# The output stage of a hybrid attention and retention block: vector, scalar and GpSimd work in written order, with lags between squares, root and scalings

## Chip, cores and metric

The kernel runs on one core of one Trainium2 chip. The metric is device time in microseconds (us) of one execution.

## What is computed

The reference is one layer of an encoder block on 2048 tokens of width 1024, in float32: an RMS norm, one wide input projection, chunked attention with a relative bias (branch A), chunkwise retention with a group norm (branch B), a gated sum of both branches, an output projection, a residual, and a last RMS norm. The change touches the end:

```python
mixed = sigmoid(m_a) * branch_a + sigmoid(m_r) * branch_r
x = x + jnp.einsum('bsd,de->bse', mixed, w_out)
return rms_norm(x, final_gain)   # x * rsqrt(mean(x*x) + 1e-6) * final_gain
```

## The kernel before

**Jobs and chunks.** All dense projections run in one stream of jobs (`p0, g0, p1, g1, ba0, ba1, br0, br1, out`). The last is `out`, the output projection: eight chunks of 256 tokens. `br1` ahead of it makes the last part of the gated sum.

**Products.** A chunk of `out` is a 2x2 block product in seven block products (a Strassen form) instead of eight. The table PRODUCTS (line 227) gives for product n its resident operand R[m], its streamed operand and its PSUM bank: 0 and 3 add into bank x, 4 and 6 into z, 1 is y, 2 is v, 5 is w. The streamed operand of 0, 3 and 6 is a block of the loaded `raw` tiles, that of 4, 1, 2, 5 a difference t1, t2, t3, t4 of such blocks, made on GpSimd (`sum`, line 332). Every operand is split into a high part `wh` (a cast on ScalarE) and the remainder `wl` (a subtraction, on VectorE, for products 2 and 5 on GpSimd; `make`, line 294). One product is 12 matmuls: high times high, high times remainder, remainder times high, for four slices. It needs `wh` at its first matmul and `wl` at its third.

**Order of products.** `ORDERS` (line 48) has the orders: "s" for chunk 0, "o" for chunks 1 to 6, "l" for chunk 7. In "o" and "l" product 4 follows product 0. In "s" of the kernel before product 3 does: both write bank x, so product 3 waits until ScalarE has copied product 0's result out (`u2`, line 381). Product 6 adds into bank z, so it waits until VectorE has read z into `c22` (line 394), for which v must be there.

**Epilogue of a chunk.** `product` (lines 369 to 398) combines the banks into four 128x512 results on VectorE; `ep_out` (line 1207) takes each: VectorE adds the residual into the tile `xr`, ScalarE squares it and sums the squares (`jk`, line 1217), GpSimd multiplies by the gain (`fg`, line 1218). When a chunk has its four sums, VectorE computes the inverse root in a chain of 13 instructions on tiles of 128x2 (lines 196 to 211 and 1227), and ScalarE scales the four `fg` tiles (line 1235), which SyncE's DMA queue writes out. In chunk 7 the root and scalings run for each half as soon as its two squares are there, and half of the scalings are VectorE's.

**What sets the order.** Work is written out by step: a product is four steps, and `later(n, fn)` (line 244) puts `fn` n steps further on. Operands are prepared three products ahead (`AHEAD`, `prime`). Matmuls and SyncE's DMAs always keep the written order. ScalarE, VectorE and GpSimd go through `Sometimes` (line 148): while `strict[0]` is true they keep the written order, otherwise a scheduler that works with estimated durations orders each engine's instructions. Line 1787 sets it to false before `ba0`, so `ba`, `br` and `out` are ordered by the scheduler. While it is false, `make` writes the remainder right behind the cast, and the differences t1 to t3 all belong to product 0 ("loose" in `SUM_AT`). Each engine runs its instructions in its order, and one that waits holds all behind it, a DMA issue on ScalarE's queue (`raw`) included.

**The start of `out`.** The operands R[0], R[1], R[3] are in place when `out` begins. R[4], R[5], R[2], R[6] still hold operands of `br1` until its last four products (n = 4 to 7 of chunk 3) are done; after each of them `place_wo` (line 1183) overwrites one, with four casts on ScalarE and four remainders (VectorE three, GpSimd one). `raw` has three buffers; chunks 0 and 1 need four, so that the fourth load waits until t3 of chunk 0 is made.

Of the kernel before, what the change touches and what calls it, by code (L numbers as in the profile page):

```python
# [21 lines left out]
P = 128  # L22
SEQ = 2048
DM = 1024
# [6 lines left out]
T = 256  # L31
WIN = 640
ROPE_BASE = 10000.0
NORM_EPS = 1e-6
GN_EPS = 1e-5
MASK = 1e30
RSQRT_MAGIC = 1597463007.0
# [6 lines left out]
ORDERS = {"p": (0, 4, 1, 2, 3, 5, 6), "g": (0, 1, 3, 2, 4, 5, 6)}  # L44
FRONT = (0, 3, 5, 1, 2, 4, 6)
ORDERS["f"] = LAST = (0, 3, 1, 2, 4, 5, 6)

ORDERS["s"], ORDERS["o"], ORDERS["l"] = (0, 3, 4, 1, 2, 5, 6), (0, 4, 1, 2, 3, 5, 6), (0, 4, 1, 2, 5, 6, 3)
AHEAD = 3
PARTS = 8  # L50
RAWS = 3
# [21 lines left out]
def hybrid_kernel(  # L73
# [24 lines left out]
    small = ctx.enter_context(tc.tile_pool(name="small", bufs=4))  # L98
# [5 lines left out]
    def r32(ap):  # L104
        return ap.bitcast(F32)
# [40 lines left out]
    strict = [True]  # L146

    class Sometimes(Ordered):
# [3 lines left out]
    pe, act, dve, pool = Ordered(nc.tensor), Sometimes(nc.scalar), Sometimes(nc.vector), Sometimes(nc.gpsimd)  # L152
# [43 lines left out]
    def rsqrt(v, y, tmp, hv):  # L196

        dve.tensor_scalar(tmp.bitcast(I32), v.bitcast(I32), 1, None, ALU.logical_shift_right)
        dve.tensor_scalar(
            y.bitcast(I32), tmp.bitcast(I32), -1.0, RSQRT_MAGIC, ALU.mult, ALU.add  # L200
        )
        dve.tensor_scalar(hv, v, -0.5, None, ALU.mult)
        if v.shape[-1] == 1:
            for _ in range(3):
                dve.scalar_tensor_tensor(tmp, y, hv, y, ALU.mult, ALU.mult)
                dve.scalar_tensor_tensor(y, tmp, 1.5, y, ALU.add, ALU.mult)
            return
        for _ in range(3):
            dve.tensor_tensor(tmp, y, hv, ALU.mult)
            dve.tensor_tensor(tmp, tmp, y, ALU.mult)  # L210
            dve.scalar_tensor_tensor(y, tmp, 1.5, y, ALU.add, ALU.mult)
# [45 lines left out]
    def put(lag, dst, src):  # L257

        later(lag, lambda: dma(dst, src))
# [10 lines left out]
    class Chunk:  # L270
# [54 lines left out]

# [3 lines left out]
    }  # L329

    class Strassen(Chunk):
# [17 lines left out]
                later(1 + 3 * k, lambda q=q: load(q))  # L349

        def sums(self, n):
            if self.b is None and self.raw:
# [112 lines left out]
    def dense(jobs):  # L465
        chunks = [ch for job in jobs for ch in job.chunks]
        following = dict(zip(chunks, chunks[1:]))
        starts = [k for k, (job, ch, n) in enumerate(seq) if isinstance(ch, Plain) and ch.at(n)[2] == 0]
        count, begins = {}, {}
        for at, (job, ch, n) in enumerate(seq):  # L470
            if isinstance(ch, Strassen):
                begins.setdefault(ch, at)
        sooner = {at - lead: (ch, [j]) for ch, at in begins.items() for j, lead in enumerate(RAW_LEADS)}
        one, two_, three = jobs[2].chunks[:3]
        for ch in (one, two_, three):
            for lead in RAW_LEADS:
                sooner.pop(begins[ch] - lead)
        two_.raw, three.raw = [], []
        at = begins[one]
        sooner[at - 9], sooner[at - 6] = (one, [0]), (one, [1])  # L480

        first_out = jobs[-1].chunks[0]
        at = begins[first_out]
        for lead in RAW_LEADS:
            sooner.pop(at - lead)
        sooner[at - 6], sooner[at - 4] = (first_out, [0]), (first_out, [1])
        operands = {begins[ch] - 2: ch for ch in begins if ch.job.before}
        for at, (job, ch, n) in enumerate(seq):
# [664 lines left out]
    wo = {}  # L1153
# [26 lines left out]
        later(10, sums)  # L1180
        later(13, rest)

    def place_wo(m):
        for k in range(4):
            def low(k=k):
                eng = pool if k == 2 else dve
                eng.tensor_tensor(R[m][1][:, k, :], wo[m, k], r32(R[m][0][:, k, :]), ALU.subtract)

            later(1 + k, lambda k=k: act.copy(R[m][0][:, k, :], wo[m, k]))
            later(2 + k, low)  # L1190
# [5 lines left out]
    rows_out = {}  # L1196

    def before_out(c, i, j):
        t = 2 * c + j
# [7 lines left out]
    def ep_out(c, i, j, src, ps):  # L1207

        t = 2 * c + j
        xr, fg = jobs[-1].chunks[c].got.pop((i, j))  # L1210

        dve.scalar_tensor_tensor(xr, src, 0.25, xr, ALU.mult, ALU.add)
# [3 lines left out]
        junk = E(f"jk_{t}_{i}", BF16)  # L1216
        act.activation(junk, xr, AF.Square, scale=DM ** -0.5, accum_out=fs[:, j, i:i + 1])
        pool.tensor_tensor(fg, xr, fg, ALU.mult)
        tiles[j, i] = fg
        last = c == SEQ // T - 1  # L1220

        js = [j] if last and {(j, 0), (j, 1)} <= set(tiles) else [0, 1] if not last and len(tiles) == 4 else []
        if not js:
            return
        n = len(js)
        ft, fr, tm, hv = (small.tile([P, n], F32, tag=f"f{k}_{n}", bufs=2, name=f"f{k}_{t}") for k in range(4))
        dve.scalar_tensor_tensor(ft, fs[:, js[0]:js[-1] + 1, 0], NORM_EPS, fs[:, js[0]:js[-1] + 1, 1], ALU.add, ALU.add)
        rsqrt(ft, fr, tm, hv)
        for k, j in enumerate(js):
            t = 2 * c + j  # L1230
            for f in range(2):
                if f and last:
                    dve.tensor_scalar(tiles[j, f], tiles[j, f], fr[:, k:k + 1], None, ALU.mult)
                else:
                    act.mul(tiles[j, f], tiles[j, f], fr[:, k:k + 1])
                dst = out[0, t * P:(t + 1) * P, 512 * f:512 * f + 512]
                if t == SEQ // P - 2 and not f:
                    act.dma_start(dst, tiles[j, f])
                else:
                    put(6, dst, tiles[j, f])  # L1240


    def attention(s, sbp, ps_wide):
# [450 lines left out]
    end, at = {}, 0  # L1694
# [4 lines left out]
    def hook(name, c, n, fn):  # L1699
        hooks.setdefault((name, c, n), []).append(fn)  # L1700
# [10 lines left out]
        hook("br1", *divmod(1 + 6 * k, 8), lambda k=k: fill_wo(k))  # L1711


    for n, m in ((4, 4), (5, 5), (6, 2), (7, 6)):
        hook("br1", 3, n, lambda m=m: place_wo(m))

    stream = [dense(jobs)]
    seq.extend((job, ch, n) for job in jobs for ch, n in job.seq)
    for j in (jobs[0], jobs[2]):
# [143 lines left out]
```

## Time and profile before

| | us |
|---|---|
| median of 3 runs (lowest, highest) | 1993.12 (1991.28, 1993.23) |
| profiled execution | 1991.35 |
| its span | 1989.6 |
| PE busy | 1913.1 (96%) |
| VectorE, GpSimd, ScalarE busy | 1422.6, 994.7, 936.9 |
| stage `out`, first to last matmul | 1801.42 to 1979.83 |
| from there to the end of the span | 9.77 |

The profile is one execution on the chip. PE is TensorE, PEld its weight loads, DVE VectorE, ACT ScalarE, POOL GpSimd, SP the SyncE queue. Rows of the timeline give start, duration, engine, line and instruction, and in brackets how long the engine had been idle and what released it. Rows that keep the written order carry the line of the wrapper, 142. A matmul's shown duration overlaps the next one's: what counts is the distance between starts.

### The profile page before, as it was taken

How to read it: one execution, taken by the hardware profiler on the slowest of the kernel's cores; microseconds unless marked ns; L12 is line 12 of the kernel's file. 1: busy time of each engine (PE TensorE's matmuls, PEld its weight loads, DVE VectorE, ACT ScalarE, POOL GpSimd, SP SyncE). 2: the span in 40 equal slices, each digit the busy share in tenths (PEclk: the TensorE clock that was granted, in tenths of full speed). 3: DMA queues.
4: the chain of work that ended last, by engine and by line, in shares of the span. 5: the costliest groups of instructions: out<-in, count | busy, mean ns of one | idle time of the engine just before them, and what ended most of it. 6: DMA issues, size and time to landing. Idle time of an engine off the chain costs nothing.

```text
span 1989.6 us, 30295 instructions
## 1 busy us (share of the span) xinstructions
PE 1913.1 (96%) x9616; PEld 1586.9 (80%) x9616; DVE 1422.6 (72%) x2582; ACT 936.9 (47%) x1893; POOL 994.7 (50%) x799
## 2 busy tenths in 40 slices
PE   6899999999999999999999999999999999999997
PEld 4777878888888887778788888888888878887775
DVE  7887878677765668888886677765656654557776
ACT  6454454566654555343334555554555322224443
POOL 2343544555546675544543444544665115557664
PEclk9999999999999999999999999999999999999999
DMA  4576796756549988667676555555998999876663
GB/s 148 158 263 185 226 300 204 208 152 183 164 122 280 294 247 279 194 226 217 189 224 199 165 162 171 151 149 157 274 280 279 337 344 339 305 247 206 202 202 109
DMA packets 335055, 434.85 MB, mean 219 GB/s; under 512 B 30040, under 2 KB 194544, under 8 KB 334896
## 3 DMA queue, kind: packets, MB, share of 16 engines
q1 hardware_dynamic: 269296, 368.68, 58.5%
q10 hardware_dynamic: 65600, 64.24, 10.6%
q8 instruction: 77, 1.26, 0.3%
q14 instruction: 82, 0.67, 0.1%
HBM read 288.21 MB, written 144.60 MB: 218 GB/s over the span
## 4 chain that ended last, share of the span: by engine, by line
PE 73%; DVE 14%; DMA 5%; issue 4%; ACT 3%; POOL 1%; SPq 1%; ACTq 0%; DVEq 0%; POOLq 0%
PE ps_g_z L142 6%; PE ps_g_x L142 6%; PE ps_p_z L142 6%; PE ps_p_x L142 5%; PE po L142 4%; PE wide L142 4%; PE ps_g_y L142 3%; PE ps_g_v L142 3%; PE ps_g_w L142 3%; PE tp L142 3%; PE o L142 3%; PE ps_p_y L142 2%; PE ps_p_w L142 2%; PE ps_p_v L142 2%; DVE u_p L142 2%
## 5 line engine op out<-in xcount | busy, mean ns | idle before, releaser
L142 POOL TENSOR_SCALAR pr<-pr,rsum 128x640 f32<-128x640 f32 (+4 forms) x128 | 96.0, 750 | 225.9 <-DVE ptl L142 105.8
L142 POOL TENSOR_TENSOR t_p<-raw_p,t_p 128x512 f32<-128x512 f32 x50 | 73.5, 1470 | 147.6 <-DVE wl_p L142 125.7
L142 PE MATMUL ps_g_z<-r,wh_g 128*128 128x512 f32 x448 | 143.2, 401 | 2.1 <-DVE c_g L142 1.9
L142 DVE CUSTOM_DVE_ANT_0 pr<-wide,bt 128x640 f32<-128x640 f32 (+4 forms) x128 | 94.3, 737 | 71.0 <-PE wide L142 63.2
L142 PE MATMUL ps_p_z<-r,wh_p 128*128 128x512 f32 x448 | 141.2, 396 | 3.2 <-DVE c_p L142 2.8
L142 PE MATMUL ps_g_x<-r,wh_g 128*128 128x512 f32 x448 | 143.1, 400 | 0.9 <-ACT u_g L142 0.9
L142 PE MATMUL ps_p_x<-r,wh_p 128*128 128x512 f32 x448 | 141.6, 397 | 1.6 <-ACT u_p L142 1.5
L142 ACT ACTIVATE pr<-pr,mn 128x640 f32<-128x640 f32 (+4 forms) x128 | 98.1, 766 | 84.9 <-DVE mn L142 84.9
L142 DVE TENSOR_TENSOR ptl<-tp,pth 128x384 fp32r<-128x384 f32 x168 | 95.9, 573 | 41.0 <-ACT pth L142 40.7
L142 ACT CAST pth<-tp 128x384 fp32r<-128x384 f32 x168 | 84.7, 515 | 70.3 <-PE tp L142 64.8
L142 POOL TENSOR_TENSOR sl<-sm,sh 128x512 fp32r<-128x512 f32 x64 | 88.8, 1387 | 49.3 <-ACT sh L142 28.8
L142 DVE TENSOR_TENSOR wl_p<-t_p,wh_p 128x512 fp32r<-128x512 f32 x112 | 104.3, 932 | 2.1 <-ACT wh_p L142 2.1
L142 PEld LDWEIGHTS ps_p_x<-r,wh_p 128*128 128x128 f32 x448 | 83.4, 190 | 19.9 <-ACT u_p L142 2.4
L142 PEld LDWEIGHTS ps_p_z<-r,wh_p 128*128 128x128 f32 x448 | 81.8, 188 | 20.1 <-issue 4.8
L142 POOL TENSOR_TENSOR wl_g<-t_g,wh_g 128x512 fp32r<-128x512 f32 x56 | 75.1, 1341 | 43.0 <-ACT wh_g L142 41.0
L142 DVE TENSOR_TENSOR sm<-sr,dm 128x512 f32<-128x512 f32 x64 | 44.1, 689 | 73.4 <-PE sr L142 35.3
L142 PE MATMUL wide<-ka,qa 128*128 128x512 f32 (+2 forms) x448 | 94.2, 326 | 2.3 <-DVE mn L142 2.3
L142 PEld LDWEIGHTS tp<-ident,pr 128*128 128x128 f32 x560 | 71.3, 140 | 27.5 <-POOL pr L142 2.2
L142 PE MATMUL po<-pth,va 128*128 128x256 f32 x336 | 93.0, 297 | 0.0
L142 ACT CAST wh_p<-t_p 128x512 fp32r<-128x512 f32 x112 | 69.2, 620 | 48.7 <-PE ps_p_z L142 22.5
L142 PE MATMUL tp<-ident,pr 128*128 128x128 f32 x560 | 89.0, 273 | 2.9 <-POOL pr L142 1.6
L142 PEld LDWEIGHTS wide<-ka,qa 128*128 128x128 f32 x448 | 75.3, 188 | 19.2 <-DVE mn L142 7.7
(886 smaller groups left out, 6060.4 us busy)
## 6 DMA issues: line engine op xcount, KB each, us to landing
raw_g<-in_w_in_dram ACTq DMA_DIRECT2D x56, 512.0 KB, 5.3
raw_p<-in_w_in_dram ACTq DMA_DIRECT2D x50, 512.0 KB, 6.2
qa<-qas SPq DMA_DIRECT2D x128, 128.0 KB, 3.0
qr<-qrs SPq DMA_DIRECT2D x128, 128.0 KB, 4.5
vr<-vrs SPq DMA_DIRECT2D x64, 256.0 KB, 5.5
ka<-kas SPq DMA_DIRECT2D x40, 256.0 KB, 3.6
va<-vas SPq DMA_DIRECT2D x40, 256.0 KB, 3.0
kds<-kdt_k SPq DMA_DIRECT2D x32, 256.0 KB, 4.3
```

Source lines behind the costliest of these rows:

```text
L142: return tc.keep_in_program_order(op(*a, **k))
```

## The change

- From `br1`, chunk 3, after n = 2 on, `strict[0]` is true again: ScalarE, VectorE and GpSimd keep the written order to the end. With it the remainders are written four steps after the casts, and t1 to t4 are spread by three new rows of `SUM_AT`.
- Order "s" has product 4 before product 3. The two `raw` loads of chunk 0 are written 8 and 5 products ahead instead of 6 and 4.
- `ep_out` is split: residual, then squares one step later, then the root (one function for all chunks, 12 instructions, its iterate `tiny` in one PSUM bank of the pool of z and w) three to six steps later, the four scalings eight to eleven steps later, output DMAs four steps after each instead of six. Chunk 7 is no longer scaled by halves: all four scalings follow its fourth square, two on ScalarE with their DMAs on ScalarE's queue, two on VectorE.
- `place_wo` takes a first step and a spacing: (1, 1) for R[4], R[5], (2, 2) for R[2], (3, 2) for R[6]; remainders two steps behind casts.

```diff
-ORDERS["s"], ... = (0, 3, 4, 1, 2, 5, 6), ...
+ORDERS["s"], ... = (0, 4, 3, 1, 2, 5, 6), ...
...
+        "s": {0: ("t1",), 3: ("t2",), 1: ("t3",), 2: ("t4",)},
+        "o": {0: ("t1", "t2"), 4: ("t3",), 3: ("t4",)},
+        "l": {0: ("t1", "t2"), 4: ("t3",), 2: ("t4",)},
...
-        sooner[at - 6], sooner[at - 4] = (first_out, [0]), (first_out, [1])
+        sooner[at - 8], sooner[at - 5] = (first_out, [0]), (first_out, [1])
...
+        def added():
+            dve.scalar_tensor_tensor(xr, src, 0.25, xr, ALU.mult, ALU.add)
+            later(1, squares)
+        def squares():
+            act.activation(junk, xr, AF.Square, scale=DM ** -0.5, accum_out=fs[:, j, i:i + 1])
+            pool.tensor_tensor(fg, xr, fg, ALU.mult)
...
+            if len(tiles) == 4:
+                finish()
+        def finish():
+            if not tiny:
+                tiny.append(TR("tiny"))
+            y = tiny[0][:, 0:2]
...
+            later(3, first)
+            for n in range(3):
+                later(4 + n, lambda n=n: newton(n))
+            for k in range(4):
+                later(8 + k, lambda k=k: scaled(k // 2, k % 2))
+        added() if ps else later(1, added)
...
+    hook("br1", 3, 2, lambda: strict.__setitem__(0, True))
-        hook("br1", 3, n, lambda m=m: place_wo(m))
+        hook("br1", 3, n, lambda n=n, m=m: place_wo(m, *((1, 1) if n < 6 else (n - 4, 2))))
```

What this does to the engines' order is shown at two places. In the names, the first number behind `out` is the chunk, the second the product or the bank; `fg_0_1` belongs to token tile 0, half 1.

ScalarE, in the second chunk (chunk 1), before: the four scalings of chunk 0 stand ahead of the cast for product 5.

```order
L298 CAST wh_out_1_3_20269<-raw_out_1_1_20013 128x512
L381 COPY u2_out_1_20265<-ps_out_1_x_20247 128x512
L1235 ACTIVATE fg_0_0_19991<-fg_0_0_19991,f1_1_20224 128x512
L1235 ACTIVATE fg_0_1_20034<-fg_0_1_20034,f1_1_20224 128x512
L1235 ACTIVATE fg_1_0_20060<-fg_1_0_20060,f1_1_20224 128x512
L1235 ACTIVATE fg_1_1_20009<-fg_1_1_20009,f1_1_20224 128x512
L298 CAST wh_out_1_5_20290<-t4_out_1_20267 128x512
L298 CAST wh_out_1_6_20308<-raw_out_1_1_20013 128x512
```

The same place after the change:

```order
L142 COPY u2_out_1_20249<-ps_out_1_x_20225 128x512
L142 CAST wh_out_1_3_20255<-raw_out_1_1_20009 128x512
L142 CAST wh_out_1_5_20281<-t4_out_1_20198 128x512
L142 ACTIVATE fg_0_0_19987<-fg_0_0_19987,fr_0_20233 128x512
L142 ACTIVATE fg_0_1_20029<-fg_0_1_20029,fr_0_20233 128x512
L142 ACTIVATE fg_1_0_20053<-fg_1_0_20053,fr_0_20233 128x512
L142 ACTIVATE fg_1_1_20006<-fg_1_1_20006,fr_0_20233 128x512
L142 CAST wh_out_1_6_20307<-raw_out_1_1_20009 128x512
```

The cast for product 5 has moved ahead of the scalings; the cast for product 6 still follows them.

GpSimd, around the start of `out`, before: t2 and t3 of chunk 0 stand ahead of the additions `gr` of `br1`, chunk 3.

```order
L340 TENSOR_TENSOR t2_out_0_19945<-raw_out_0_1_19923,t1_out_0_19943 128x512
L340 TENSOR_TENSOR t3_out_0_19947<-raw_out_0_0_19885,raw_out_0_1_19923 128x512
L1148 TENSOR_TENSOR gr_6_2_19806<-gr_6_2_19806,ta_6_2_19807 128x512
L1148 TENSOR_TENSOR gr_6_3_19849<-gr_6_3_19849,ta_6_3_19850 128x512
L1187 TENSOR_TENSOR r41_90<-ws2_2_19631,r40_89 128x512
```

After the change t3 stands behind three of these additions and one remainder of R[4]:

```order
L1151 TENSOR_TENSOR gr_6_2_19806<-gr_6_2_19806,ta_6_2_19807 128x512
L142 TENSOR_TENSOR t1_out_0_19910<-raw_out_0_0_19849 128x512
L142 TENSOR_TENSOR gr_6_3_19851<-gr_6_3_19851,ta_6_3_19852 128x512
L142 TENSOR_TENSOR t2_out_0_19948<-raw_out_0_1_19908,t1_out_0_19910 128x512
L142 TENSOR_TENSOR gr_7_2_19890<-gr_7_2_19890,ta_7_2_19891 128x512
L142 TENSOR_TENSOR r41_90<-ws2_2_19631,r40_89 128x512
L142 TENSOR_TENSOR t3_out_0_19978<-raw_out_0_0_19849,raw_out_0_1_19908 128x512
```

And on ScalarE after the change the fourth `raw` load, which waits for t3, stands eight places ahead of the copy that frees bank x:

```order
L142 DMA raw_out_1_1_20009<-mxs_0_430 128x4x256
L142 CAST wh_out_0_3_20011<-raw_out_0_1_19908 128x512
L142 CAST r20_85<-wo_1_1_0_19361 128x512
L142 CAST r20_85<-wo_1_1_1_19494 128x512
L142 CAST wh_out_0_1_20040<-t2_out_0_19948 128x512
L142 CAST r20_85<-wo_1_1_2_19627 128x512
L142 CAST r60_93<-ws4_0_19367 128x512
L142 CAST r20_85<-wo_1_1_3_19760 128x512
L142 COPY u2_out_0_20065<-ps_out_0_x_20043 128x512
```

Before, that load stood ahead of the cast for product 3, and the sixteen casts of the resident operands followed, as the copy did.

More of the change, by code (lines that the diff above doesn't have):

```diff
@@ L46 @@
 ORDERS["f"] = LAST = (0, 3, 1, 2, 4, 5, 6)
-ORDERS["s"], ORDERS["o"], ORDERS["l"] = (0, 3, 4, 1, 2, 5, 6), (0, 4, 1, 2, 3, 5, 6), (0, 4, 1, 2, 5, 6, 3)
+ORDERS["s"], ORDERS["o"], ORDERS["l"] = (0, 4, 3, 1, 2, 5, 6), (0, 4, 1, 2, 3, 5, 6), (0, 4, 1, 2, 5, 6, 3)
 AHEAD = 3
@@ L351, in sums @@
         def sums(self, n):
-            if self.b is None and self.raw:
+            if self.b is None and len(self.raw or ()) == 2:
                 self.b = {f"b{j + 1}{c + 1}": self.half(j, c) for j in range(2) for c in range(2)}
@@ L1181, in fill_wo, with place_wo @@
         later(13, rest)
-    def place_wo(m):
+    def place_wo(m, first, every):
         for k in range(4):
@@ L1187, in low @@
                 eng.tensor_tensor(R[m][1][:, k, :], wo[m, k], r32(R[m][0][:, k, :]), ALU.subtract)
-            later(1 + k, lambda k=k: act.copy(R[m][0][:, k, :], wo[m, k]))
-            later(2 + k, low)
+            later(first + every * k, lambda k=k: act.copy(R[m][0][:, k, :], wo[m, k]))
+            later(first + every * k + 2, low)
     def mx_stream(c, j):
@@ L1194, in mx_stream @@
         return mxscr[b][4 * j:4 * j + 4, :, T * u:T * u + T].rearrange("k p t -> p k t")
-    rows_out = {}
+    rows_out, tiny = {}, []
     def before_out(c, i, j):
@@ L1210, in ep_out @@
         xr, fg = jobs[-1].chunks[c].got.pop((i, j))
-        dve.scalar_tensor_tensor(xr, src, 0.25, xr, ALU.mult, ALU.add)
         if c not in rows_out:
@@ L1215, in ep_out @@
         tiles, fs = rows_out[c]
[L1216 to L1231, printed above, removed]
+        def added():
+            dve.scalar_tensor_tensor(xr, src, 0.25, xr, ALU.mult, ALU.add)
+            later(1, squares)
+        def squares():
+            junk = E(f"jk_{t}_{i}", BF16)
+            act.activation(junk, xr, AF.Square, scale=DM ** -0.5, accum_out=fs[:, j, i:i + 1])
+            pool.tensor_tensor(fg, xr, fg, ALU.mult)
+            tiles[j, i] = fg
+            if len(tiles) == 4:
+                finish()
@@ new lines, in finish, with first, newton, scaled @@
+        def finish():
+            if not tiny:
+                tiny.append(TR("tiny"))
+            y = tiny[0][:, 0:2]
+            r, tmp, v = (small.tile([P, 2], F32, tag=f"f{n}", bufs=2, name=f"f{n}_{c}") for n in "rtv")
+            def first():
+                dve.scalar_tensor_tensor(v, fs[:, :, 0], NORM_EPS, fs[:, :, 1], ALU.add, ALU.add)
+                dve.tensor_scalar(tmp.bitcast(I32), v.bitcast(I32), 1, None, ALU.logical_shift_right)
+                dve.tensor_scalar(y.bitcast(I32), tmp.bitcast(I32), -1.0, RSQRT_MAGIC, ALU.mult, ALU.add)
+            def newton(n):
+                dve.scalar_tensor_tensor(tmp, y, -0.5, v, ALU.mult, ALU.mult)
+                dve.tensor_tensor(tmp, tmp, y, ALU.mult)
+                dve.scalar_tensor_tensor(r if n == 2 else y, tmp, 1.5, y, ALU.add, ALU.mult)
+            def scaled(j, f):
+                a, w = tiles[j, f], r[:, j:j + 1]
@@ L1232, in ep_out @@
                 if f and last:
-                    dve.tensor_scalar(tiles[j, f], tiles[j, f], fr[:, k:k + 1], None, ALU.mult)
+                    dve.tensor_scalar(a, a, w, None, ALU.mult)
                 else:
[L1235 to L1238, printed above, removed]
-                else:
-                    put(6, dst, tiles[j, f])
+                    act.mul(a, a, w)
@@ new lines, in scaled @@
+                dst = out[0, (2 * c + j) * P:(2 * c + j + 1) * P, 512 * f:512 * f + 512]
+                if last and not f:
+                    act.dma_start(dst, a)
+                else:
+                    put(4, dst, a)
+            last = c == SEQ // T - 1
+            later(3, first)
[4 more added lines that the diff above has]
+        added() if ps else later(1, added)
```

## The prediction

> **What bounds the kernel now.** PE is busy for 96% of the span, so a gain can only come from the places where it is not. I cut the stage `out` at the first matmul of each chunk and asked for the busy times by stretch (columns: stretch; length, then busy us of PE, PEld, DVE, ACT, POOL; granted clock; DMA share; GB/s).
>
> ```profile
> 1801.42:1824.33 22.91, 20.17 (x85) 15.46 (x84) 18.73 (x20) 7.36 (x15) 17.39 (x12) 1.00 0.76 239
> 1824.33:1846.18 21.85, 19.61 (x86) 15.62 (x84) 16.94 (x29) 9.91 (x22) 15.17 (x11) 1.00 0.45 147
> 1846.18:1869.50 23.32, 21.22 (x85) 16.74 (x84) 18.42 (x29) 9.88 (x21) 15.32 (x12) 0.93 0.64 205
> ...
> 1889.60:1911.28 21.68, 19.64 (x86) 15.61 (x84) 16.69 (x28) 9.52 (x21) 14.30 (x11) 1.00 0.62 196
> 1911.28:1934.56 23.28, 21.23 (x85) 16.78 (x84) 18.17 (x29) 9.85 (x21) 15.00 (x12) 0.93 0.64 208
> ...
> 1955.59:1979.83 24.24, 21.07 (x85) 16.63 (x83) 16.89 (x29) 8.71 (x19) 11.77 (x9) 0.93 0.18 66
> 1979.83:1989.60 9.77, 0.00 (x0) 0.00 (x0) 5.54 (x23) 2.17 (x4) 1.34 (x2) 0.67 0.29 107
> ```
>
> What a chunk should take comes from the chain of waits, where a product runs undisturbed:
>
> ```profile
> 1872.39 2.72 PE ps_out_z L142 x12
> ```
>
> Twelve matmuls take 2.72 us, so a chunk of seven products takes 19.04. Chunk 0 loses 22.91 - 19.04 = 3.87; chunks 1 to 6, from 1824.33 to 1955.59, lose 131.26 - 114.24 = 17.0; chunk 7 loses 24.24 - 19.04 = 5.20. Together that is 26 us, and 9.77 follow the last matmul. The table of waits names PE's releasers (columns: us, count, mean):
>
> ```profile
> PE ps_out_w L142 <- ACT wh_out L298: 6.0, 4, 1.6
> PE ps_out_w L142 <- POOL wl_out L299: 3.7, 6, 0.6
> PE ps_out_z L142 <- DVE c_out L394: 3.6, 2, 3.2
> PE ps_out_x L142 <- ACT u_out L381: 1.0, 1, 1.0
> ```
>
> Product 5 (w) waits for its cast and then for its remainder. Of the 17.0 these waits name 6.0 + 3.7; chunks 2 and 5, with a granted clock of 0.93, are each about 1.5 longer than their neighbours with 1.00; the other 4.3 hides in matmuls whose ends are modelled. Why the cast is late is in the timeline of chunk 4 (start, duration, engine, work, idle time and releaser in brackets):
>
> ```profile
> 1895.47 0.38 DVE L1227 SCALAR_TENSOR_TENSOR f<-fs 128x2 f32<-128x2 f32 x1 [0.79 <-ACT jk L1217]
> 1895.88 1.23 DVE L198 TENSOR_SCALAR f<-f 128x2 int32<-128x2 int32 x1
> ...
> 1901.67 2.56 ACT L1235 ACTIVATE fg<-fg,f 128x512 f32<-128x512 f32 x4 [5.24 <-DVE f L211]
> ...
> 1904.81 1.27 POOL L299 TENSOR_TENSOR wl_out<-t_out,wh_out 128x512 fp32r<-128x512 f32 x1 [5.11 <-ACT wh_out L298]
> ...
> 1904.79 0.73 PE L142 MATMUL ps_out_w<-r,wh_out 128*128 128x512 f32 x2 [1.43 <-ACT wh_out L298]
> ...
> 1906.13 0.50 PE L142 MATMUL ps_out_w<-r,wl_out 128*128 128x512 f32 x1 [0.61 <-POOL wl_out L299]
> ```
>
> ScalarE stood idle for 5.24 us at the four scalings, which wait for the root; the cast for product 5 stands behind them, and GpSimd, idle 5.11 us, and PE wait for that cast. The same chain strikes chunk 7 through product 6: ScalarE's cast comes late, VectorE waits 3.14 us for it with `c22` behind, and PE waits 3.17.
>
> ```profile
> 1969.15 0.69 DVE L299 TENSOR_TENSOR wl_out<-raw_out,wh_out 128x512 fp32r<-128x512 f32 x1 [3.14 <-ACT wh_out L298]
> ...
> 1972.52 0.84 PE L142 MATMUL ps_out_z<-r,wh_out 128*128 128x512 f32 x2 [3.17 <-DVE c_out L394]
> ...
> 1976.92 0.62 PE L142 MATMUL ps_out_x<-r,wh_out 128*128 128x512 f32 x2
> ```
>
> There the wait also costs clock: the product behind it takes 1976.92 - 1972.52 = 4.40 instead of 2.72, 1.68 more. In chunk 2 a shorter wait did so too, at a granted clock of 0.93 for the chunk:
>
> ```profile
> 1861.42 0.73 PE L142 MATMUL ps_out_w<-r,wh_out 128*128 128x512 f32 x2 [1.48 <-ACT wh_out L298]
> ```
>
> The Trainium skill ("TensorE: Matmul & The Clock Gate", "What's actually happening") has the clock fall only after a window of about 3.4 us without work; chunk 2 shows it after 1.48, so the measurement decides, and by the rule a stall in chunk 0 would cost its length alone, 1.7 less in the upper bound of that chunk.
>
> **The change part by part.** *Cast ahead of scalings, chunks 1 to 6.* With the cast for product 5 free of the root, PE's wait goes; what is late next must be worked out. T is a chunk's first matmul. In chunk 4 the chain began 1895.47 - 1889.60 = T + 5.87; in written order I place it at T + 4.2. Its length is open, as before shows it in SBUF only and the new iterate lies in PSUM. Nearest are these small instructions with a PSUM operand early in the program (ns at the end of x3: min/median/max):
>
> ```profile
> L142 DVE SCALAR_TENSOR_TENSOR n_b<-tiny,n_b x3: 161/161/161, 30.5 to 31.7; 128x4 f32<-128x4 f32 x3
> L142 DVE TENSOR_TENSOR n_b<-n_b,tiny x3: 157/157/158, 30.7 to 31.9; 128x4 f32<-128x4 f32 x3
> ```
>
> From start to start I estimate 0.2 us each; one of the first two has no PSUM operand and may take 1.23. So the chain takes 0.38 + 1.23 + 10 x 0.2 = 3.6 and ends at T + 7.8, or T + 9.5 from 5.87. Behind it on VectorE stands the remainder for product 3, at most 1.78 by this row:
>
> ```profile
> 1891.20 1.78 DVE L299 TENSOR_TENSOR wl_out<-t_out,wh_out 128x512 fp32r<-128x512 f32 x1
> ```
>
> It is ready at T + 9.6 (11.3 at the latest) and wanted at the third matmul of the fifth product, 4 x 2.72 + 0.45 = T + 11.3. The scalings run from T + 7.8 for 2.56 to 10.4, the cast for product 6 ends near T + 11.0, and product 6 starts at T + 16.3: there the new wait on ScalarE has 5 us of cover. GpSimd has ten operations a chunk; they take 1.29 or 1.75, the longer beside VectorE's work, and the loads they wait for 8.0:
>
> ```profile
> 1898.42 1.29 POOL L1218 TENSOR_TENSOR fg<-xr,fg 128x512 f32<-128x512 f32 x1
> ...
> 1894.09 1.75 POOL L340 TENSOR_TENSOR t_out<-raw_out 128x512 f32<-128x512 f32 x1
> ```
> ```profile
> raw_out<-mxs ACTq DMA_DIRECT2D x12, 512.0 KB, 8.0
> ```
>
> In written order GpSimd does the last two gains by T + 5.2, the remainder for product 2 by 6.9 (wanted at 8.6), t1 and t2 of the next chunk by 8.7 and 10.4, and the remainder for product 5 by 12.2 (wanted at 5 x 2.72 + 0.45 = 14.05). The loads for t1, t2 are issued near T + 16.5 and 17.9 of the chunk before and land at T + 5.5 and 6.9, in time. Each slack is 1.7 to 1.8 us, all at the slow durations, so I count no wait: 17.0 us gained. The other bound is 1.5 us left in each of six chunks, 9.
>
> The Trainium skill ("GPSIMD Engine Reference", "Key points") speaks against the change: GpSimd shares its SBUF interface with VectorE and contends with it. The trace agrees (1.29 and 1.75). By it a fuller VectorE and GpSimd slow each other, yet an iterate in PSUM would spare the chain; by the rule the sum would be between B's 1974 and 1984, or D's where the chain is struck.
>
> *Chunk 0.* Product 3 comes third instead of second, so PE wants the copy of bank x 2.72 us later. But the fourth `raw` load waits for t3, which now stands behind three additions `gr` and a remainder, and ScalarE holds seven casts and the copy that frees bank x behind that load.
>
> ```profile
> 1796.91 0.32 SPq L142 DMA_DIRECT2D ta<-tas  x1
> ```
> ```profile
> DMA to landing us min/median/max: 2.5/3.2/3.8
> ```
> ```profile
> 1794.59 4.27 ACT L1189 CAST r<-ws 128x512 fp32r<-128x512 f32 x8
> ```
> ```profile
> 1804.63 0.58 ACT L381 COPY u_out<-ps_out_x 128x512 f32<-128x512 f32 x1
> ...
> 1805.27 0.74 PE L142 MATMUL ps_out_x<-r,wh_out 128*128 128x512 f32 x2 [0.97 <-ACT u_out L381]
> ```
>
> The last `ta` lands at 1796.91 + 3.2 = 1800.1 (1799.4 to 1800.7); addition, remainder and t3 at up to 1.75 each end at 1805.4 (I take 1805.1; 1803.2 to 1805.9). Seven casts of 4.27 / 8 = 0.53 follow, to 1808.9 or with the issue 1809.2, and the copy to 1809.8. PE wants bank x for the third product at 1801.42 + 5.44 = 1806.86: it waits 2.9 us (1.0 to 3.8), and some 0.5 to 1 for a remainder behind. That is 3.9, what the chunk loses now, so I put it at zero; the bounds are 4 gained (no wait at all) and 3 lost (3.8 + 1.0 + 1.7 of clock, less 3.9).
>
> *Chunk 7.* The cast for product 6 stands ahead of chunk 6's scalings; `c22` follows v (done at T + 10.9) by two operations and is wanted at T + 13.6. The 3.17 of wait, 1.68 of clock and 0.19 around them go: 5.04 of the 5.20; 0.16 is the last matmul's end.
>
> *Tail.* P is 1979.83, the end of the window of chunk 7.
>
> ```profile
> 1981.19 0.63 ACT L1217 ACTIVATE jk<-xr 128x512 bf16<-128x512 f32 x1 [1.89 <-DVE xr L1212]
> ...
> 1985.43 0.72 ACT L1235 ACTIVATE fg<-fg,f 128x512 f32<-128x512 f32 x1 [1.46 <-DVE f L206]
> 1986.18 0.36 ACTq L1238 DMA_DIRECT2D out_dram<-fg  x1
> ```
>
> The last square ends at P + 2.0. Then come twelve small instructions, 2.4; scaling 0.72, issue 0.36, scaling 0.72: the last issue at P + 6.2, against P + 6.35 now. But four outputs of 256 KB leave together instead of two and two. I take 0; bounds 0.3 gained, 0.8 lost. On SyncE's queue an output now stands four steps, 2.72 us, behind its scaling instead of six; behind it stand only loads for later chunks, and the scalings end by T + 10.4, so nothing is held: zero, and the wait of one late scaling if that cover goes.
>
> *Sum*: 17.0 + 5.04 + 0 + 0 = 22.1. Against the profiled execution, 1991.35, that is 1969.3. The median of the runs, 1993.12, lies 1.77 higher and gives 1971.1. I predict **1970**.
>
> **The rivals.** *B: GpSimd sets the pace.* For it: ten operations at 1.75 are 17.5 us of 19.04, and in chunk 4 it waited at two of them,
>
> ```profile
> 1909.27 2.55 POOL L1218 TENSOR_TENSOR fg<-xr,fg 128x512 f32<-128x512 f32 x2 [1.48 <-DVE xr L1212]
> ```
> ```profile
> 1890.76 1.67 POOL L340 TENSOR_TENSOR t_out<-raw_out,t_out 128x512 f32<-128x512 f32 x1 [0.63 <-DVE wl_out L299]
> ```
>
> so 17.5 + 1.48 + 0.63 = 19.6, 0.57 over PE; times seven 4 us, 1974. With one more wait of 1.48 it is 21.1, 14.4 us, 1984. Against it: GpSimd's busy time was 14.3 to 15.3 a chunk. Between them, 1977.
>
> *C: chunk 0 does not wait.* If t3 comes at the early end, 1966.
>
> *D: slower.* If every instruction of the chain takes 1.23, as the one in SBUF above, the chain is 12 x 1.2 = 14.4 long and ends at T + 18.6; the remainder for product 3 behind it is ready at 20.4, 9 us late in six chunks: 1970 + 54 = 2024. It decides where PE loses more than the 22 us gained, 3.7 a chunk: a chain that ends later than T + 11.3 - 1.8 + 3.7 = 13.2 and is over 9 us long, 7 of 12 instructions at 1.23. Against it: 157 to 161 ns in the rows with PSUM.
>
> *E: it does not do what it says.* If product 5's wait came from t4 on GpSimd and not from the order on ScalarE, it would stay: 1989 to 1993. The 5.11 us that GpSimd stood idle speak against it.
>
> **How the numbers follow.** Forecast 0.62 (its own range 1966 to 1973.5: chunk 0 and tail), B 0.20, C 0.09, D 0.04, E 0.05. The range 1966 to 1980 holds the forecast, C and most of B. A measurement tells 0.2%, about 4 us, from no change: faster is the forecast, B and C, 0.91; same is E, 0.05; slower is D, 0.04.
>
> **What would show it.** Right: in the profile after, chunks 1 to 6 at 19.0 to 19.4 us each at clock 1.00; no wait of w on the cast; a chain with at most two instructions over 1 us; chunk 7 at 19.2; in chunk 0 a wait of 1 to 4 us on bank x's copy. Wrong: GpSimd above 17 us in a chunk with PE waiting on its remainder (B); VectorE's chain over 9 us with product 3 waiting (D); a wait of w on the cast as long as now (E); a tail above 11.

## The result, and the profile after

The changed kernel takes 1974.22 us (median of 5 runs, 1970.05 to 1980.61), against 1993.21 before (5 runs): the ratio is 0.9904, interval 0.9881 to 0.9928, or 19 us. The profiled execution took 1975.88, its span 1974.2. By stretch, from the first matmul of a chunk to that of the next (same columns as before):

```profile
1805.24:1830.84 25.60, 21.26 (x86) 16.76 (x84) 22.02 (x21) 10.80 (x22) 21.85 (x14) 0.93 0.72 240
1830.84:1849.88 19.04, 19.04 (x86) 15.77 (x84) 15.65 (x28) 10.24 (x22) 15.60 (x11) 1.00 0.57 186
...
1887.96:1907.00 19.04, 19.04 (x86) 15.77 (x84) 14.25 (x26) 9.87 (x22) 14.01 (x11) 1.00 0.72 222
...
1945.08:1964.12 19.04, 19.04 (x85) 15.58 (x83) 13.20 (x25) 8.25 (x19) 9.19 (x8) 1.00 0.17 63
1964.12:1974.20 10.08, 0.16 (x1) 0.00 (x0) 3.92 (x15) 2.17 (x4) 1.53 (x2) 0.77 0.28 104
```

Chunks 1 to 7 take 19.04 us each, seven products of 2.72 with nothing lost. Chunk 0 takes 25.60, 2.69 more than before. From the first matmul of `out` to the end of the span it is 168.96 us (before: 188.18), 19.2 less; this stretch is the measure below. PE's waits in it, complete:

```profile
PE ps_out_x L142 <- ACT u_out L142: 3.7, 1, 3.7
PE ps_out_z L142 <- DVE c_out L142: 0.6, 1, 0.6
```

Product 5 waits no more. In the chunk that starts at 1887.96, VectorE's root chain and ScalarE's cast and scalings stand like this:

```profile
1891.68 0.60 DVE L142 SCALAR_TENSOR_TENSOR fv<-fs 128x2 f32<-128x2 f32 x1 [0.79 <-ACT jk L142]
1892.31 1.23 DVE L142 TENSOR_SCALAR ft<-fv 128x2 int32<-128x2 int32 x1
1893.57 0.16 DVE L142 TENSOR_SCALAR tiny<-ft 128x2 int32<-128x2 int32 x1
...
1895.32 0.16 DVE L142 SCALAR_TENSOR_TENSOR fr<-ft,tiny 128x2 f32<-128x2 f32 x1
```
```profile
1893.42 0.62 ACT L142 CAST wh_out<-t_out 128x512 fp32r<-128x512 f32 x1 [0.79 <-PE ps_out_z L142]
1895.51 2.57 ACT L142 ACTIVATE fg<-fg,fr 128x512 f32<-128x512 f32 x4 [1.47 <-DVE fr L142]
```

The chain runs from T + 3.72 to T + 7.52, where T is the chunk's first matmul (predicted: 4.2 to 7.8). It takes 3.8 us and one instruction is over 1 us, although GpSimd works nearly all the time:

```profile
1892.21 1.30 POOL L142 TENSOR_TENSOR wl_out<-t_out,wh_out 128x512 fp32r<-128x512 f32 x1
1893.46 1.30 POOL L142 TENSOR_TENSOR t_out<-raw_out 128x512 f32<-128x512 f32 x1
1894.84 1.29 POOL L142 TENSOR_TENSOR t_out<-raw_out,t_out 128x512 f32<-128x512 f32 x1
```

Before, the chain of chunk 4 took 6.1 us: three of its 13 instructions are over 1 us, and the scheduler had put a remainder of 0.68 into it. The second and the third of these three, beside what GpSimd did, and the chain's last:

```profile
1897.35 1.13 DVE L209 TENSOR_TENSOR f<-f,f 128x2 f32<-128x2 f32 x1
1898.51 1.21 DVE L210 TENSOR_TENSOR f<-f,f 128x2 f32<-128x2 f32 x1
...
1901.41 0.16 DVE L211 SCALAR_TENSOR_TENSOR f<-f,f 128x2 f32<-128x2 f32 x1
```
```profile
1897.16 1.30 POOL L340 TENSOR_TENSOR t_out<-raw_out,t_out 128x512 f32<-128x512 f32 x1
```

After the change the cast for product 5 is done 1.47 us before the scalings begin.

The whole time of the changed kernel scatters by over 10 us between its runs, and part of the scatter arises long before this stretch. Ahead of `ba0` both kernels run the same instructions in the same order, but there the first matmul of the second group of input projections starts at 777.99 in the profile of before,

```profile
777.99 0.39 PE L142 MATMUL ps_p_x<-r,wh_p 128*128 128x512 f32 x1
```

and at 782.35 in that of after:

```profile
782.35 0.62 PE L142 MATMUL ps_p_x<-r,wh_p 128*128 128x512 f32 x2
```

In the experiments it lies between 776.5 and 783.3. So the stages of the traces are compared below, and the whole times beside them.

### The profile page after: what moved, and what is told of

Its sections match the earlier page's. It is cut to its first block, busy times and chain, and to the rows that moved or that the text cites. A ratio compares the mean times of both kernels' runs of the same rounds, so it can differ in the third digit from the quotient of the medians.

```text
span 1974.2 us, 30273 instructions
## 1 busy us (share of the span) xinstructions
PE 1906.4 (97%) x9616; PEld 1586.6 (80%) x9616; DVE 1399.1 (71%) x2567; ACT 938.7 (48%) x1893; POOL 993.1 (50%) x799
```

## The experiments

The theory under test after the result, "short chain": PE no longer waits because the chain is short, and it is short because its iterate lies in PSUM. The rival, "order alone": it is the place of the cast ahead of the scalings, or the written order as such. The table has the measure for each kernel (one profile each), chunk 0 in it, and the ratio of whole times to before.

| kernel | first matmul of `out` to end | chunk 0 | ratio (interval) |
|---|---|---|---|
| before | 188.18 | 22.91 | 1 |
| after | 168.96 | 25.60 | 0.9904 (0.9881 to 0.9928) |
| iterate in SBUF | 180.53 | 25.35 | 0.9954 (0.9932 to 0.9976) |
| scalings early | 168.57 | 24.82 | 0.9900 (0.9885 to 0.9914) |
| both | 183.79 | 25.25 | 0.9977 (0.9963 to 0.9991) |
| scheduler to the end | 167.78 | 23.48 | 0.9887 (0.9871 to 0.9904) |
| t3 early | 168.05 | 24.72 | 0.9900 (0.9885 to 0.9915) |
| load on SyncE | 167.35 | 24.02 | 0.9898 (0.9876 to 0.9919) |
| old order of chunk 0 | 169.80 | 26.25 | 0.9913 (0.9898 to 0.9927) |
| old epilogue | 188.63 | 29.49 | 0.9998 (0.9988 to 1.0008) |
| before, iterate in PSUM | 169.13 | 22.68 | 0.9910 (0.9893 to 0.9927) |
| load behind the third | 171.50 | 28.18 | one run |
| scheduler for chunk 0 | 167.39 | 23.90 | 0.9899 (0.9882 to 0.9915) |
| the same, load on SyncE | 167.94 | 23.89 | 0.9904 (0.9886 to 0.9922) |

**Iterate in SBUF.**

```diff
-                tiny.append(TR("tiny"))
+                tiny.append(small.tile([P, 4], F32, tag="tiny", bufs=1, name="tiny"))
```

> The changed kernel with the iterate of the root in SBUF instead of PSUM, nothing else. Measure: from the first matmul of out to the end of the span, 188.2 us before and 169.0 after in the profiles. Theory 'short chain' (the gain rests on the chain of 12 small instructions being 3.8 us long, which it is because each has an operand in PSUM and GpSimd does not slow it): GpSimd works from T+3.1 to T+11.3 of a chunk, so about six of the twelve take 1.2 us, the chain ends near T+12.3 instead of T+7.5, the remainder for product 3 behind it is 2.2 to 2.8 us late in six chunks: 182 to 188, most of the gain gone. Theory 'order alone' (the cast ahead of the scalings did it, the place of the iterate is worth nothing): 169, chunks 1 to 6 at 19.04.

Measured: 180.53, ratio 0.9954. Chunks 1 to 6 lose 11.8 us, a little less than the 13 to 19 that I expected, and where I expected it: product 3 waits for its remainder, which stands behind the chain.

```profile
PE ps_out_x L142 <- DVE wl_out L142: 8.4, 6, 2.0
```

The chain takes 7.9 us in each of these chunks, with five of its twelve instructions over 1 us. Part of one, beside what GpSimd did at the same time:

```profile
1897.74 1.22 DVE L142 TENSOR_SCALAR ft<-fv 128x2 int32<-128x2 int32 x1
1899.00 1.22 DVE L142 TENSOR_SCALAR tiny<-ft 128x2 int32<-128x2 int32 x1
1900.25 0.16 DVE L142 SCALAR_TENSOR_TENSOR ft<-tiny,fv 128x2 f32<-128x2 f32 x1
...
1900.84 1.15 DVE L142 SCALAR_TENSOR_TENSOR ft<-tiny,fv 128x2 f32<-128x2 f32 x1
1902.02 1.21 DVE L142 TENSOR_TENSOR ft<-ft,tiny 128x2 f32<-128x2 f32 x1
```
```profile
1897.65 1.29 POOL L142 TENSOR_TENSOR wl_out<-t_out,wh_out 128x512 fp32r<-128x512 f32 x1
1898.89 1.30 POOL L142 TENSOR_TENSOR t_out<-raw_out 128x512 f32<-128x512 f32 x1
1900.68 1.29 POOL L142 TENSOR_TENSOR t_out<-raw_out,t_out 128x512 f32<-128x512 f32 x1 [0.49 <-DMA raw_out<-mxs]
1901.93 1.29 POOL L142 TENSOR_TENSOR wl_out<-t_out,wh_out 128x512 fp32r<-128x512 f32 x1
```

Add start and duration: the four over 1 us end at 1898.96, 1900.22, 1901.99 and 1903.23, GpSimd's at 1898.94, 1900.19, 1901.97 and 1903.22. The instruction at 1900.25 falls where GpSimd stood idle and takes 0.16. A slow instruction is a fast one that waited for the end of a GpSimd instruction. The Trainium skill ("SBUF — State Buffer", "SBUF: two separate sides") has it so: VectorE and GpSimd share a pair of ports as an exclusive lock, which a VectorE instruction with two inputs in SBUF, or in a mode that uses two ports, takes for its whole length, and who comes second waits; the trace agrees, to 0.03 us.

**Scalings early.** The lag of the scalings is cut so that they stand between the casts for products 3 and 5 again, where they stood before the change.

```diff
-                later(8 + k, lambda k=k: scaled(k // 2, k % 2))
+                later(7, lambda k=k: scaled(k // 2, k % 2))
```

> The changed kernel with the four scalings written 7 steps after the last square instead of 8 to 11, which puts them on ScalarE behind the cast for product 3 and ahead of the cast for product 5, as before the change; the iterate stays in PSUM. Theory 'short chain': the chain still ends at T+7.5, the scalings at T+10.1, the cast at T+10.7, product 5 wants it at T+13.6: no wait, 169.0 as after. Theory 'order alone': the waits of product 5 come back, 1.6 + 0.6 us in most chunks and 1.5 of clock in some, 15 to 20 us in all: 184 to 189.

Measured: 168.57, no loss in chunks 1 to 6. ScalarE in the chunk that starts at 1887.77:

```profile
1896.53 2.56 ACT L142 ACTIVATE fg<-fg,fr 128x512 f32<-128x512 f32 x4 [2.94 <-DVE fr L142]
1899.00 0.61 ACT L142 CAST wh_out<-t_out 128x512 fp32r<-128x512 f32 x1
```

The cast is behind the scalings as before the change, and done at T + 11.8, in time for product 5 at T + 13.6. So "order alone" falls: with a short chain the place of the cast is worth nothing here.

**Both.** The two edits above together.

> Both: iterate in SBUF and the scalings ahead of the cast for product 5. Theory 'short chain': the remainder for product 3 is late as with the iterate in SBUF alone and the cast for product 5 comes near T+15.5, 1.9 late against T+13.6 but inside the delay that product 3 has already made: 183 to 190, at most 5 us more than the iterate in SBUF alone. Theory 'order alone': as with the scalings early alone, 184 to 189, and clearly more than the iterate in SBUF alone, which it puts at 169.

Measured: 183.79, 3.3 more than with the iterate in SBUF alone. Chunks 1 to 6 lose 11.4, no more than there; chunk 7 loses 3.8 where the other lost nothing: the cast for product 6 stands behind the scalings and `c22` behind that (wait 1.92, then a product of 4.41). "Short chain" holds within its bounds.

**Old epilogue.** The changed kernel with `ep_out` of before: written order without lags, iterate in SBUF.

> The changed kernel with the epilogue of before (iterate in SBUF, 13 instructions, no lags, chunk 7 by halves): written order without the lags. The chain then stands ahead of the remainder for product 1 on VectorE, and the scalings ahead of the cast for product 2 on ScalarE. Theory 'lags and short chain are the gain': the remainder for product 1 is 4 us late or more and the cast for product 2 as well, 4 to 7 us lost in each of chunks 1 to 7: 195 to 218 from the first matmul to the end, slower than before the change (188.2). Theory 'written order is the gain': 169 to 175.

Measured: 188.63, ratio 0.9998. Written order with the old epilogue gains nothing in all, but it isn't the loss of 7 us or more that I expected. Chunks 1 to 7 lose 15.3 us instead of 22.1, and chunk 0 loses 10.45 instead of 3.87, which takes that gain away. Chunks 2 to 7 lose 2.2 to 2.5 each at products 1 and 2:

```profile
PE ps_out_y L142 <- DVE wl_out L142: 5.1, 7, 0.9
PE ps_out_v L142 <- POOL wl_out L142: 4.8, 7, 0.7
```

I had the chain slowed by GpSimd; but in this order GpSimd's next work stands behind the scalings and so behind the chain itself:

```profile
1902.96 1.28 POOL L142 TENSOR_TENSOR wl_out<-t_out,wh_out 128x512 fp32r<-128x512 f32 x1 [5.36 <-issue]
```

So GpSimd is idle for 5.36 us from 1897.6 on, and in that time the chain's instructions on SBUF are fast too (two in a row here, and the last):

```profile
1897.93 0.36 DVE L142 TENSOR_TENSOR f<-f,f 128x2 f32<-128x2 f32 x2
...
1899.50 0.16 DVE L142 SCALAR_TENSOR_TENSOR f<-f,f 128x2 f32<-128x2 f32 x1
```

The chain takes 3.7 us here, no longer than after the change, and yet these chunks lose 2.2 to 2.5 us. So a short chain is not enough by itself: in written order it must also stand late enough not to hold the remainder for product 1 and, through the scalings, the cast for product 2. By the waits above the lags do that; no run has the lags alone.

**Scheduler to the end.** The line that returns to written order is left out.

> The changed kernel without the line that returns to written order: the scheduler orders ScalarE, VectorE and GpSimd to the end, with the new epilogue, lags and order of chunk 0. It too puts the cast for product 5 ahead of the scalings now. Theory 'lags': chunks 1 to 6 at 19.0 to 19.3, chunk 7 near 19.2; 165 to 171, chunk 0 losing 3 to 7 us by itself. Theory 'written order is needed': chunks 1 to 6 lose 1 to 3 us each again, 176 to 188.

Measured: 167.78. Chunks 1 to 6 lose nothing, chunk 7 1.0, chunk 0 4.4. With the new epilogue, written order is not needed.

**Before, iterate in PSUM.** The crucial one: the kernel before, with the iterate of chunks 0 to 6 moved and nothing else.

```diff
+            y = tiny[0][:, 0:2]
+            dve.tensor_scalar(tm.bitcast(I32), ft.bitcast(I32), 1, None, ALU.logical_shift_right)
+            dve.tensor_scalar(y.bitcast(I32), tm.bitcast(I32), -1.0, RSQRT_MAGIC, ALU.mult, ALU.add)
+            dve.tensor_scalar(hv, ft, -0.5, None, ALU.mult)
+            for r in range(3):
+                dve.tensor_tensor(tm, y, hv, ALU.mult)
+                dve.tensor_tensor(tm, tm, y, ALU.mult)
+                dve.scalar_tensor_tensor(fr if r == 2 else y, tm, 1.5, y, ALU.add, ALU.mult)
```

> The kernel before with one thing changed: the iterate of the root of chunks 0 to 6 lies in a PSUM tile; 13 instructions, no lags, the scheduler to the end, chunk 7 by halves as before. (The scheduler, whose estimates change with it, now puts the cast for product 5 ahead of the scalings by itself.) Measure: from the first matmul of out to the end of the span, 188.2 us before, 169.0 after the change. Theory 'short chain': it is nearly the whole gain; the chain ends near T+10 instead of T+12, chunks 1 to 6 at 19.04 to 19.3, chunk 7 near 20: 166 to 170. Theory 'lags and order are needed as well': half of the loss or more stays, 176 to 186.

Measured: 169.13, ratio 0.9910, not to be told from the whole change (0.9904). By stretch, chunks 0, 1 and 7 and the tail:

```profile
1800.37:1823.05 22.68, 20.19 (x85) 15.46 (x84) 18.49 (x20) 6.91 (x14) 17.40 (x12) 1.00 0.77 242
1823.05:1842.09 19.04, 19.04 (x85) 15.75 (x84) 14.79 (x28) 9.65 (x21) 14.97 (x11) 1.00 0.48 135
...
1938.10:1959.52 21.42, 19.29 (x85) 15.50 (x83) 15.67 (x29) 8.72 (x19) 11.63 (x9) 1.00 0.28 103
1959.52:1969.50 9.98, 0.17 (x1) 0.00 (x0) 5.75 (x23) 2.17 (x4) 1.54 (x2) 0.69 0.28 105
```

Chunks 1 to 6 lose 0.8 us together instead of 17.0, chunk 7 2.4 instead of 5.0. The chain takes 4.8 us, a remainder of 1.36 in its middle included, with one instruction over 1 us, and ends at T + 11.0. The scheduler also moved the cast ahead of the scalings by itself in this kernel, so it alone can't part the two; the run with the scalings early does. What the rest of the change adds: 2.4 in chunk 7 and 0.8 in chunks 1 to 6, less 2.9 given back in chunk 0, net 0.2.

**Chunk 0.** Its 6.56 us over 19.04 are 3.89 in front of product 3, 1.38 of half clock in it (4.10 instead of 2.72), and 1.3 at products 1, 5 and 6. PE waits for the copy of bank x, which ScalarE brings late:

```profile
1809.84 0.37 ACTq L142 DMA_DIRECT2D raw_out<-mxs  x1
1810.30 0.62 ACT L142 CAST wh_out<-raw_out 128x512 fp32r<-128x512 f32 x1 [4.69 <-POOL r L142]
...
1813.94 0.57 ACT L142 COPY u_out<-ps_out_x 128x512 f32<-128x512 f32 x1
```
```profile
1814.57 0.74 PE L142 MATMUL ps_out_x<-r,wh_out 128*128 128x512 f32 x2 [3.72 <-ACT u_out L142]
```

The profile puts ScalarE's wait down to a GpSimd remainder (`r`) that ended at the same moment; the runs below show another cause. The load goes out at out + 4.60 (4.60 us after the first matmul of `out`), and seven casts of 0.52 stand between it and the copy, which ends at + 9.27. But t3, for which I had it wait, ended at out + 2.90. So t3 was made early:

```diff
-        "s": {0: ("t1",), 3: ("t2",), 1: ("t3",), 2: ("t4",)},
+        "s": {0: ("t1",), 3: ("t2", "t3"), 2: ("t4",)},
```

> The changed kernel with t3 of chunk 0 made right behind t2 on GpSimd, ahead of an addition gr and a remainder. After the change chunk 0 takes 25.60 us, 6.56 over 19.04, with 3.72 of wait for the copy that frees bank x. Theory 'load waits for t3' (the fourth raw load, which waits for t3 to free its buffer, holds the casts and the copy on ScalarE): the load goes out about 4 us earlier, the wait falls under 1 us, chunk 0 takes 20 to 22, 164 to 166 from the first matmul to the end. Rival 'load waits for an earlier transfer' (what holds the load is one of the transfers issued before it, near out + 0 to 1 us, that lands 4 to 5 us later): the load is issued at out + 4 to 5 us as after, the wait stays 3 to 4 us, 168 to 170.

Measured: 168.05, the wait 2.28. In three other kernels whose chunk 0 is that of after, it is 2.42, 3.21 and 3.51, so the run shows no gain beyond the scatter. The trace decides (out begins at 1806.55 here): GpSimd's t3, ScalarE's load, and the transfer of `mxs` that SyncE issued at 1804.70, with its time to landing:

```profile
1802.72 1.74 POOL L142 TENSOR_TENSOR t_out<-raw_out,raw_out 128x512 f32<-128x512 f32 x1
```
```profile
1810.27 0.37 ACTq L142 DMA_DIRECT2D raw_out<-mxs  x1
1810.73 0.62 ACT L142 CAST wh_out<-raw_out 128x512 fp32r<-128x512 f32 x1 [4.43 <-DMA mxs<-gr]
```
```profile
DMA to landing us min/median/max: 5.5/5.5/5.5
```

t3 was done 5.8 us before the load went out; the write of `mxs` landed at 1810.2, and the load followed. It does so in all seven kernels with this order of transfers: issued 0.1 us after that write has landed, 4.5 to 6.0 after the write's issue. My step "waits for t3" is wrong.

To take the load from ScalarE altogether:

```diff
-                (dma if self.job.resident else act.dma_start)(raw, self.job.stream(self.c, j))
+                (dma if self.job.resident or (self.job.name, self.c, j) == ("out", 1, 1) else act.dma_start)(raw, self.job.stream(self.c, j))
```

> The changed kernel with the second raw load of chunk 1 on SyncE's queue instead of ScalarE's, so that no cast or copy stands behind it, whatever it waits for. If the hold of ScalarE by this load is what costs chunk 0 its wait: bank x's copy is free by out + 5 us, the wait falls to 0 to 0.6, no clock is lost, chunk 0 takes 19.5 to 21.5 and the whole 163.5 to 166. If the sixteen casts of the resident operands are the limit by themselves: the wait stays at 2 us or more, 167 to 170. A price may come on SyncE's queue: what stands behind the load there goes out later, which no matmul waits for.

Measured: 167.35, chunk 0 24.02, over what I expected. The copy is done at out + 3.5 and the wait for bank x is gone, but VectorE's remainders take its place (the three longest waits):

```profile
PE ps_out_y L142 <- DVE wl_out L142: 2.0, 1, 2.0
PE ps_out_z L142 <- DVE c_out L142: 0.7, 1, 0.7
PE ps_out_x L142 <- DVE wl_out L142: 0.6, 1, 0.6
```

So the load held ScalarE, and behind that the twelve remainders of resident operands on VectorE hold PE: of 6.56 lost, only 1.6 come back.

Then the old order of products alone in chunk 0:

```diff
-ORDERS["s"], ... = (0, 4, 3, 1, 2, 5, 6), ...
+ORDERS["s"], ... = (0, 3, 4, 1, 2, 5, 6), ...
```

> The changed kernel with chunk 0 in the old order of products (0, 3, 4, ...). Product 3 then wants bank x one product earlier, at out + 2.72 instead of 5.44, while the copy comes near out + 9.3: the wait grows by about 2.7 us from 3.72 to 6.4, and the whole from 169.0 to 171.5 to 172. Rival, that the order of chunk 0 is worth nothing since other waits of the chunk (remainders of the resident operands on VectorE) take its place: 169 to 170.

Measured: 169.80, a wait of 4.87 and a chunk of 26.25: the total is the rival's, though the wait did grow. Chunk 0 takes 24.82 to 25.60 in the kernels that have it as after, so the new order is worth 0.7 to 1.4, not 2.7: the copy itself came at out + 7.7 here against 9.3, since the `mxs` write landed after 4.5 us instead of 5.7.

What the load waits for, if neither t3 nor data (the load reads another tensor of the `mxs` set than this write fills), was tried in one run, with t3 early and the load written directly behind the third:

```diff
+        second = begins[jobs[-1].chunks[1]]
+        sooner.pop(second - 8)
+        sooner[second - 9] = (jobs[-1].chunks[1], [0, 1])
```

> The changed kernel with t3 of chunk 0 made early (as in the run with t3 early, where the fourth raw load went out at out + 3.7 us although t3 was done at out - 2.1) and that load written directly behind the third, so that another transfer stands ahead of it in the rotation of the eight completion semaphores: by the listing it is the last load of ta, no longer the write of mxs. Theory 'the load waits for the transfer that last used its semaphore': it is issued when that ta lands, near out + 0.5 to 1.5 us. Theory 'the load waits for the write of mxs as data': it stays at out + 3 to 4.6. If it waits for nothing but t3: near out - 2.

Measured: the load went out at out + 3.3, which none of the three gives. It did not wait for t3, nor for the `mxs` write, which landed at out + 4.7 here. The two `raw` loads (the second starts at 1809.85) and the last `ta`:

```profile
1804.32 5.90 ACTq L142 DMA_DIRECT2D raw_out<-mxs  x2
```
```profile
1804.90 0.32 SPq L142 DMA_DIRECT2D ta<-tas  x1
```

The semaphores in the traces settle it. The program has eight semaphores on which transfers report that they have landed, and ahead of the load's issue ScalarE's queue waits for the one that the load itself will report on. In this run it is the one that the last `ta` used before it: its sixteen reports end at 1809.75, 4.85 us after the issue of that `ta`, and the load goes out 0.1 us later. In the changed kernel it is the one that the `mxs` write used: reports end at out + 4.50, load at out + 4.59. So the first theory has the cause right; its time was wrong because it had the `ta` land 2.2 to 3.2 us after its issue. Why `ta` took longer here is open.

**A better beginning.** The return to written order put off into chunk 0, and the same with the load on SyncE:

```diff
-    hook("br1", 3, 2, lambda: strict.__setitem__(0, True))
+    hook("out", 0, 5, lambda: strict.__setitem__(0, True))
```

> The changed kernel with the return to written order put off to product 5 of chunk 0 of out: the scheduler orders the beginning of out, the written order the rest. Chunk 0 as in the run with the scheduler to the end (23.5 us, 2.1 less than after), chunks 1 to 7 at 19.04: 166.5 to 167.5 from the first matmul to the end, 1.5 to 2.5 us less than after. If the borrowed order of chunk 0 does not fit what follows: 168 to 171.

> The same with the second raw load of chunk 1 on SyncE's queue as well. If this load still holds ScalarE at the beginning of out: chunk 0 under 23 us, 165 to 166.5. If VectorE and GpSimd (22 us of work each in chunk 0) set chunk 0 already: 166.5 to 167.5, no change against the run before.

Measured: 167.39 and 167.94, chunk 0 23.90 and 23.89, the others 19.04. Both gain 1 to 1.6 us on the change in this stretch; the whole times (0.9899, 0.9904) can't tell that, and the second adds nothing: there VectorE and GpSimd set chunk 0. None of these kernels beats the change by more than the measurement tells.

## Why the prediction was right, and where it was not

Predicted were 1970 us, 1966 to 1980, and 22.1 us gained; measured are 1974.22 and, in the traces, 19.2. In the table chunk 7 ends and the tail begins with the end of the last matmul, as in the prediction, 0.16 us past the last window above.

| term | predicted | measured |
|---|---|---|
| chunks 1 to 6 | 17.0 | 17.0 |
| chunk 7 | 5.04 | 5.04 |
| chunk 0 | 0 (4 gained to 3 lost) | 2.69 lost |
| tail | 0 (0.3 gained to 0.8 lost) | 0.15 lost |

*Chunks 1 to 6* came out to the tenth, and the times within the chunk nearly so. But the step's reason was half wrong. It said that the wait goes "with the cast for product 5 free of the root". The cast is free, and with the scalings back ahead of it nothing is lost. What counts is the length of the chain, which the step carried as an unknown: 3.6 us, from rows with a PSUM operand early in the program. The same sum would have been wrong by 12 us with the iterate in SBUF, and right to 0.8 us in the kernel before with its iterate in PSUM, without written order and lags. In written order the place of the chain counts as well (old epilogue: 3.7 us long, and 15.3 us lost in chunks 1 to 7).

*Rival D* was that case: its mechanism is real and was avoided by the place of the iterate. Its price, 54 us, was too high: five of the twelve instructions are slow in the chunk shown, not all, since GpSimd has gaps, and the cost is 11.8. That chain, 7.9 us long and ending at T + 12.2, stays below the line that D drew for a slower kernel (over 9 us, T + 13.2), and the kernel is indeed still faster than before.

*Rival C* did not happen: chunk 0 waited.

*Rival B*, GpSimd's pace, did not happen: 14.0 us a chunk in the steady state, not 17.5, and in most operations 1.29. The 1.75 was an upper bound taken as the usual.

*Rival E*: written order with the old epilogue gains nothing in all, but the change is more than that.

*Chunk 0* is the term that was mis-sized. The wait on the copy, 3.72, lies at the end of its bounds (1.0 to 3.8), and the 1.7 of clock that I kept for the bound only did come, as 1.38. The step that failed is "the fourth `raw` load waits for t3". t3 ended at out + 2.90, 0.8 us earlier than reckoned, and the load went out 1.7 us after it: it waited for the `mxs` write, landed at out + 4.50, whose semaphore it shares. That the loss still lies inside the bounds is luck, since no term of theirs came from that write.

*Clock.* Where product 3 ran slowly in chunk 0, the granted clock over it was low: 0.68 after the change, 0.62 with the scalings early. Behind waits in the same place product 3 took 4.10 after 3.72 us (after the change), 4.44 after 2.42 (scalings early), 2.89 after 3.21 (both) and 2.85 after 2.28 (t3 early). The length of a wait alone doesn't say whether it costs clock. The Trainium skill ("TensorE: Matmul & The Clock Gate", "What's actually happening") has the clock fall after one idle window of about 3.4 us; 2.42 lies under it and cost clock, so the measurement decides.

*Tail*: the last output is issued 6.23 us after the last matmul's end (predicted 6.2, before 6.35), and the span ends 3.69 us after that issue, against 3.42 before. That the 6.2 fits is partly luck: the last square ended 0.6 us earlier than reckoned, and chain and scalings took as much longer. What is lost lies behind the issue, 0.2 of it in the landing of this output (2.7 us instead of 2.5); that this comes from four outputs leaving together is argued, not shown:

```profile
1970.51 0.36 ACTq L142 DMA_DIRECT2D out_dram<-fg  x1
```

## What to carry to other kernels

When a chain of tiny instructions holds an engine's queue, look at the durations of its single instructions before its order: a few of 1.2 us among many of 0.16 point to a shared resource, and one operand in another memory can be worth the whole rewrite. Check a rewrite of many parts by putting its smallest part alone into the old kernel. Where whole times scatter by 5 to 10 us, compare the stage.

## What the runs showed of the hardware that was not expected

- A 128x2 VectorE instruction on SBUF takes 0.16 us, or waits for the end of GpSimd's current instruction, up to 1.23; with its iterate in PSUM it takes 0.16 beside a busy GpSimd.
- The issue of a load on ScalarE's queue was held with all casts behind it, and ScalarE idle for 4.7 us, until a write by another queue to another place had landed: the program gives the load the same completion semaphore.
- In `out`, large GpSimd operations take 1.29 us, or up to 1.75 beside a VectorE remainder or residual, and such a VectorE operation up to 1.78 instead of 0.68: each delays the other.
